# Three placements in a streaming mixer-and-experts kernel: where a register load stands, the order of a ring of buffers, and how far ahead splits run

## The chip, the cores and the metric

The kernel runs on one core of a Trainium2 chip. The metric is device microseconds (us) of one execution; the median of several runs is given. All times inside an execution come from one profiled execution and are counted from the start of its span.

## The reference, cut to what matters

One layer of a streaming encoder for 512 frames of 1024 features, in float32. Three mixers (differential attention, a gated delta rule, a diagonal state-space model) read one input projection; one output projection and a layer norm follow. Then a router picks, for each frame, one group of four experts and two experts in it, and the chosen experts of 16 gated MLPs are summed:

```python
def hier_moe(h, w_grp, b_grp, w_exp, b_exp, w1, w3, w2):
    ...
    for e in range(N_EXPERTS):
        hid = jax.nn.silu(hf @ w1[e]) * (hf @ w3[e])
        out = out + comb[:, e:e + 1] * (hid @ w2[e]).astype(jnp.float32)
```

`comb` is zero but for two experts of each frame, so an expert needs only the frames that chose it. A last layer norm ends the layer.

## The kernel before, in words

**Two halves.** The first half (to about 480 us) is the mixers, the output projection, the first layer norm (its result goes to two DRAM tensors, `hdr` and `yd`) and the routing. The routing ends in `place`, which writes tables of frame numbers and weights (`tab`), the numbers of the experts in the order in which they will run (`placed`, inside the tile `sb16`), and `cnti`, the largest number of frames that any expert has left over after its list. The second half runs the 16 experts, each on a list of at most 128 frames (large) or 64 (small). Expert 0, 1 and 2 are large; the 13 others follow as SSLSLSSLSLSLL, S for small and L for large, so nine are large and seven small.

**Weights.** An expert has 12 chunks of 128x1024 float32 (512 KB): eight "up" chunks, four "down" chunks. All 192 are loaded in order by SyncE (SP) into a ring of 32 places, `NRAW`. A place is a fixed stretch of SBUF that belonged to tiles of the first half; its first load must wait until the last user of those tiles has finished. Which place is used first, second, and so on is the tuple `RING`. SP issues in program order, so one load that waits holds back all loads behind it. A later load into a place waits for the chunk that was there 32 loads before. Load 29 is made to wait for the first two gathers (`FIRST = 28`).

**Splits.** A chunk of a large expert is split on the chip into a high part (`e_hi`, ScalarE) and a low part (`e_lo`, VectorE); three matmuls with the high and low parts of the frames (`xth`, `xtl`) stand for one float32 product. Split chunks lie in a ring of eight tiles, that is four chunks (`NHL = 8`). Chunks of small experts are used as they are loaded. `ahead(i, casts)` is called before step `i` (one chunk of PE work) and writes loads and splits into the program; how many steps a split may precede its use is `casts + AHEAD`, with `casts` 4 (2 in the last 12 steps), and no more than four splits are ever waiting. ScalarE and VectorE execute their instructions in program order, so where a split is written decides what waits behind it: `hid` (the activation of the previous expert) and `xth` and `xtl` (the next expert's frames) are on the same two engines.

**Frames.** POOL gathers the frames of an expert from `hdr` (`xg`), TensorE turns them, and adds the result to `yd` by an indirect DMA (`yd<-y,tab`). The last two experts are added on the chip, before the last layer norm.

**The register load.** Lines 1859 and 1860 load `cnti` into a register of every engine and branch, where an expert has frames left, into code that handles them. The load is written at the end of the program, outside the parts whose order is fixed by hand; the scheduler puts it, on each engine, by what it depends on. It depends on the write of `cnti` in line 289.

Of the kernel before, what the change touches and what calls it, by code (L numbers as in the profile page):

```python
# [16 lines left out]
ALU = mybir.AluOpType  # L17
AX = mybir.AxisListType
# [23 lines left out]
NQ4 = 4  # L42
RING = (2, 8, 15, 14, 21, 13, 12, 11, 9, 10, 5, 29, 7, 30, 18, 31, 16, 17, 19, 20, 6, 27, 28, 0, 1, 3, 4, 22, 23, 24, 25, 26)
OHT = 20
HT = 9
PRE = (4, 4, 9)
# [2 lines left out]
LAG = 2  # L49
CASTS = 4  # L50
CASTS2 = 2
AHEAD = 4
SW = 12
POOL = 4
NORM = 'vvvv'
# [4 lines left out]
NE = 16  # L60
# [21 lines left out]
def tile_layer(ctx: ExitStack, tc: tile.TileContext, a, out):  # L82
    nc = tc.nc

    def tt(o, x, y, op, e=nc.vector):
        return e.tensor_tensor(o, x, y, op=op)  # L86

    def ts(o, x, s1, op0, s2=None, op1=None, e=nc.vector):
        if op1 is None:
            return e.tensor_scalar(o, x, s1, None, op0=op0)  # L90
        return e.tensor_scalar(o, x, s1, s2, op0=op0, op1=op1)  # L91

    def stt(o, x, s, y, op0, op1):
        return nc.vector.scalar_tensor_tensor(o, x, s, y, op0=op0, op1=op1)  # L94
# [7 lines left out]
    def mm(o, l, r, start=True, stop=True):  # L102
        return nc.tensor.matmul(o, l, r, start=start, stop=stop)  # L103
# [34 lines left out]
    def ones_tile(shape, name, v=1.0):  # L138
        o = const.tile(shape, F32, name=name)
        nc.gpsimd.memset(o, v)  # L140
        return o
# [24 lines left out]
    sb16 = ones_tile([P, P], "sb16")  # L166
# [41 lines left out]
    cnti = const.tile([P, 1], I32, name="cnti")  # L208
# [24 lines left out]
        nc.vector.tensor_reduce(tab[1], p, axis=AX.X, op=ALU.add)  # L233


    more0, half2 = sb16[:, 0:NE], sb16[:, 32:33]
    placed = sb16.bitcast(I32)[:, 16:16 + ND]

    fold2 = stri
# [17 lines left out]
    def place(p, ct, pd, a, b):  # L257

        key, sl, red = a[:, 0:NE], a[:, 16:48].rearrange("p (x e) -> p x e", x=2), a[:, 64:64 + 2 * ND]
        rank, no = a[:, 96:96 + ND], a[:, 112:112 + NE]  # L260
        red = red.rearrange("p (x r) -> p x r", x=2)
        gt = a[:, 128:128 + ND * ND].rearrange("p (r e) -> p r e", e=ND)
        oh = a[:, 300:300 + ND * ND].rearrange("p (r e) -> p r e", e=ND)
        x = b[:, 0:2 * ND * ND].rearrange("p (x r e) -> p x r e", x=2, e=ND)
        sq, dyn = [P, ND, ND], slice(NS, NE)
        stt(key, ct, 16.0, i16, ALU.mult, ALU.subtract)
        tt(gt, key[:, None, dyn].to_broadcast(sq), key[:, dyn, None].to_broadcast(sq), ALU.is_gt)
        nc.vector.tensor_reduce(rank, gt, axis=AX.X, op=ALU.add)
        tt(oh, i16[:, 0:ND, None].to_broadcast(sq), rank[:, None, :].to_broadcast(sq), ALU.is_equal)
        tt(gt, oh, i16[:, None, dyn].to_broadcast(sq), ALU.mult)  # L270
        nc.vector.tensor_reduce(no[:, 0:ND], gt, axis=AX.X, op=ALU.add)
        nc.vector.tensor_copy(placed, no[:, 0:ND])
        ts(more0[:, dyn], rank, NL - 0.5, ALU.is_gt, float(SL - P), ALU.mult)
        for q, c in enumerate((slice(0, 2), slice(2, 5))):
            nc.vector.tensor_reduce(sl[:, q], p[:, :, c], axis=AX.X, op=ALU.add)
        mm(pd[:, 0:2 * NE], fold2, a[:, 16:48])
        ts(tab[0][:, 2:NS], sl[:, 0, 2:NS], 4096.0, ALU.add)
        nc.vector.tensor_copy(tab[1][:, 0:NS], sl[:, 1, 0:NS])
        pd = pd[:, 0:2 * NE].rearrange("p (x e) -> p x e", x=2)
        for r, y in ((slice(0, NL), sl), (slice(NL, ND), pd)):  # L280
            n = [P, 2, r.stop - r.start, ND]
            tt(x[:, :, r], y[:, :, None, dyn].to_broadcast(n), oh[:, None, r].to_broadcast(n), ALU.mult)
        nc.vector.tensor_reduce(red, x, axis=AX.X, op=ALU.add)
        ts(tab[0][:, NS:NS + NL], red[:, 0, 0:NL], 4096.0, ALU.add)
        ts(tab[0][:, NS + NL:], red[:, 0, NL:], 2.0, ALU.mult, half2, ALU.add)
        nc.vector.tensor_copy(tab[1][:, NS:], red[:, 1])
        tt(no, ct, more0, ALU.subtract)
        nc.vector.tensor_reduce(key[:, 0:1], no, axis=AX.X, op=ALU.max)
        nc.vector.tensor_copy(cnti, key[:, 0:1])


    def rsqrt(o, x, n, pool, eps, scale=1.0):
# [1170 lines left out]
    def halves(p):  # L1463
        return [p[:, 0:512], p[:, 512:D]]
# [3 lines left out]
    def traw(dt=F32):  # L1468
        nraw[0] += 1
        return rp[RING[(nraw[0] - 1) % NRAW]].tile([P, D], dt, name="e_raw", tag="raw")  # L1470

# [24 lines left out]
    def at(i, e):  # L1496
        return tab[i][:, column[e]:column[e] + 1]
# [20 lines left out]
    def turn_x(xg, e=0):  # L1518
        if small[e]:
            p = psT()  # L1520
            for j in range(4):
                nc.tensor.transpose(p[:, j * P:(j + 1) * P], xg[:, j * P:(j + 1) * P], ident)
            x = exs("xth", F32, 2)
            act(x, p, AF.Copy)
            return x
        return [turn(xg[:, i * 512:(i + 1) * 512], "xt", 2) for i in range(2)]
# [62 lines left out]
    def gather_for(e):  # L1589
        return gather(xgs[e % 2][:, 0:512] if small[e] else xgs[e % 2], at(0, e), 1 + small[e])  # L1590
# [24 lines left out]
    def ahead(i, casts):  # L1615
        while len(raws) < min(i + NRAW + 1, N):
            raws.append(traw())
            x = nc.sync.dma_start(raws[-1], weights(*steps[len(raws) - 1]))
            if len(raws) == FIRST + 1:

                for y in first:
                    tc.add_manual_dep(x.ins, y.ins.name, mybir.DependencyInfo(
                        mybir.DependencyClass.Sync, mybir.DependencyReason.DATA), reason="room")
        while len(ws) < min(i + casts + AHEAD, N):
            n = len(ws)
            if small[steps[n][0]]:
                ws.append(raws[n])
            elif n < i + casts or (nsplit[0] < nused[0] + casts and n < N - SW):
                ws.append(split(raws[n]))
                nsplit[0] += 1  # L1630
            else:
                break

    def step(i):
        e, c = steps[i]
        b = e % 2
        nused[0] += not small[e]
        if c < 8:
            if c == 0:
                pp[e] = psA(b)  # L1640
                if e + 2 < NE:
                    gather_for(e + 2)
            if small[e]:
                if c % 2:
                    up2(pp[e][0], xts[e], c // 2, ws[i - 1:i + 1])
            else:
                up(pp[e][c % 2], xts[e], c, ws[i])
                if c == 6:
                    hid[e] = hidden(pp[e])
            if c == 7:  # L1650
                if small[e]:
                    hid[e] = exs("hid", F32)
                    act(hid[e][0:SL], pp[e][0][0:SL], AF.Silu)
                    tt(hid[e][0:SL], pp[e][0][SL:P], hid[e][0:SL], ALU.mult)
                else:
                    tt(hid[e], pp[e][1], hid[e], ALU.mult)
                if e + 1 < NE:
                    xts[e + 1] = turn_x(xgs[(e + 1) % 2], e + 1)
                if e == 0:
                    turn_h(e)  # L1660
        else:
            if c == 8:
                pys[e] = psA(1 - b) if e == NE - 1 else psS()
            if small[e]:
                down2(pys[e][0], hts[e], c - 8, ws[i])
            else:
                down(pys[e], hts[e], c - 8, ws[i])
            if e == NE - 2 and c == HT:
                turn_h(e + 1)
            if c == 11:  # L1670
                if e + 1 < NE - 1:
                    turn_h(e + 1)
                if e < NE - 2:
                    (finish2 if small[e] else finish)(pys[e][0] if small[e] else pys[e], at(1, e), at(0, e))
                else:
                    y_parts(e)
# [17 lines left out]
    with tc.manual_schedule():  # L1694
        first.extend(gather_for(e) for e in range(2))
        ahead(0, CASTS)
        xts[0] = turn_x(xgs[0])
        for i in range(N - 4):
            ahead(i + 1, CASTS if i < N - SW else CASTS2)
            step(i)  # L1700
            if i == N - OHT:
                io = traw()[:, 0:S]
                gp.iota(io, pattern=[[1, S]], base=0, channel_multiplier=0, allow_small_or_imprecise_dtypes=True)
                oht.extend(halves(traw(F32R)))
                for j in range(2):
                    nc.vector.tensor_copy(li[j], at(0, NE - 2 + j))
                    ts(oht[j], io, li[j], ALU.is_equal)


    with tc.manual_schedule():  # L1710
# [265 lines left out]
```

## Time and profile before

| what | value |
|---|---|
| median of 3 runs | 814.47 us (812.86 to 816.69) |
| the profiled execution's own time | 810.5 us |
| its span, first to last instruction | 808.8 us |
| mean granted TensorE clock | 0.908 of full |
| TensorE matmuls busy | 695.3 us (86%) |
| VectorE (DVE) busy | 526.0 us (65%) |
| ScalarE (ACT) busy | 354.7 us (44%) |

The shares are means over two halves with different limits, so they say little by themselves. What limits a stretch has to be read from that stretch: which wait ends last there, and whether the DMA engines are full or empty.

### The profile page before, as it was taken

The numbers are of one execution on the slowest core, as the hardware profiler recorded it, in microseconds if no ns is written. First come the engines' busy times: TensorE is split into PE (matmuls) and PEld (weight loads), VectorE is DVE, ScalarE is ACT, GpSimd is POOL, SyncE is SP. The second block draws the span as 40 slices with busy tenths as digits, with TensorE's granted clock in tenths as the row PEclk, the third lists the DMA queues.
The fourth block names the chain that finished last, engine by engine and source line by source line (L and its number), as shares of the span: only waits on it lengthen the run. The fifth ranks groups of instructions, "written<-read, shape, count | busy, mean of one in ns | idle before, by whom it ended". The sixth has DMA issues, their size and how long they took to land. (4 is left out here: it accounts for less than half of the span.)

```text
span 808.8 us, 10863 instructions
## 1 busy us (share of the span) xinstructions
PE 695.3 (86%) x3568; PEld 504.5 (62%) x3568; DVE 526.0 (65%) x1405; ACT 354.7 (44%) x582; POOL 97.4 (12%) x140
## 2 busy tenths in 40 slices
PE   0999939997997999998999656899899859989793
PEld 0677827875885766676877555685556326736661
DVE  6999896678534455667568885792544233816866
ACT  2678625532115221545323205674544333726643
POOL 6010000000000011110000020012212102211022
PEclk9999969998979999596899756999999989999897
DMA  6133212121012575263000249999999999999822
GB/s 216 64 111 103 81 42 78 41 79 31 22 49 69 149 177 170 64 196 105 1 0 1 105 149 401 419 404 399 359 398 390 391 382 383 388 368 385 330 94 108
DMA packets 54272, 155.77 MB, mean 193 GB/s; under 512 B 13502, under 2 KB 13758, under 8 KB 54208
## 3 DMA queue, kind: packets, MB, share of 16 engines
q1 hardware_dynamic: 38960, 124.26, 39.8%
q0 software_dynamic: 8192, 18.86, 8.9%
q10 hardware_dynamic: 7056, 11.88, 4.8%
q8 instruction: 30, 0.49, 0.2%
q14 instruction: 34, 0.28, 0.1%
HBM read 139.98 MB, written 18.61 MB: 196 GB/s over the span
## 5 line engine op out<-in xcount | busy, mean ns | idle before, releaser
L86 DVE TENSOR_TENSOR e_lo<-e_raw,e_hi 128x1024 fp32r<-128x1024 f32 x108 | 131.4, 1239 | 93.6 <-ACT e_hi L97 91.3
L97 ACT ACTIVATE e_hi<-e_raw 128x1024 fp32r<-128x1024 f32 x108 | 112.6, 1060 | 89.3 <-DMA e_raw<-in_moe_w_dram 65.7
L103 PE MATMUL pA<-hTh,w_lo 128*128 128x512 f32 x184 | 76.3, 416 | 12.3 <-DVE w_lo L86 12.3
L103 PE MATMUL pA<-hTh,w_hi 128*128 128x512 f32 x184 | 77.5, 421 | 2.5 <-DVE cv L94 1.1
L103 PE MATMUL pA<-hTl,w_hi 128*128 128x512 f32 x184 | 74.6, 406 | 0.0
L103 PE MATMUL pA<-e_hi,xth 128*128 128x512 f32 x144 | 61.2, 425 | 6.2 <-ACT xth L97 6.2
L103 PE MATMUL pA<-e_hi,xtl 128*128 128x512 f32 x144 | 60.3, 419 | 0.6 <-DVE xtl L86 0.6
L103 PE MATMUL pA<-e_lo,xth 128*128 128x512 f32 x144 | 59.7, 415 | 0.6 <-DVE e_lo L86 0.6
L103 PE MATMUL pA<-e_raw,xth 128*64 128x512 f32 x224 | 53.9, 598 | 2.1 <-DMA e_raw<-in_moe_w_dram 2.1
L103 PEld LDWEIGHTS pA<-hTh,w_lo 128*128 128x128 f32 x184 | 36.1, 196 | 20.4 <-DVE w_lo L86 12.9
L1486 POOL DMA_INDIRECT yd__140<-y,tab x14 | 23.2, 1660 | 202.2 <-ACT y L97 202.2
L97 ACT ACTIVATE w_hi<-w_raw 128x1024 fp32r<-128x1024 f32 x29 | 30.6, 1055 | 33.8 <-PE pA L103 25.0
L103 PEld LDWEIGHTS pA<-hTh,w_hi 128*128 128x128 f32 x184 | 36.0, 196 | 12.5 <-issue 2.1
L103 PEld LDWEIGHTS pA<-hTl,w_hi 128*128 128x128 f32 x184 | 35.8, 195 | 7.6 <-issue 0.7
L103 PEld LDWEIGHTS pA<-e_raw,xth 128*64 128x64 f32 x224 | 16.8, 136 | 34.0 <-issue 23.1
L103 PEld LDWEIGHTS pA<-e_hi,xth 128*128 128x128 f32 x144 | 29.5, 205 | 13.3 <-ACT xth L97 6.6
L86 DVE TENSOR_TENSOR w_lo<-w_raw,w_hi 128x1024 fp32r<-128x1024 f32 x29 | 35.3, 1220 | 2.4 <-ACT w_hi L97 2.3
L103 PEld LDWEIGHTS pA<-e_lo,xth 128*128 128x128 f32 x144 | 29.4, 204 | 7.6 <-DVE e_lo L86 1.0
L103 PEld LDWEIGHTS pA<-e_hi,xtl 128*128 128x128 f32 x144 | 29.4, 204 | 7.2 <-DVE xtl L86 1.1
L1201 DVE TENSOR_REDUCE nm<-pA 128x1 f32<-128x128 f32 (+3 forms) x48 | 22.9, 484 | 13.8 <-PE pA L103 9.0
L97 ACT ACTIVATE pe<-pA,nm 128x128 f32<-128x128 f32 (+3 forms) x48 | 25.0, 527 | 11.9 <-DVE nm L1201 7.2
L97 ACT ACT_TABLE_LOAD x21 | 26.9, 1283 | 6.7 <-DVE cv L94 6.4
(525 smaller groups left out, 1475.1 us busy)
## 6 DMA issues: line engine op xcount, KB each, us to landing
e_raw<-in_moe_w_dram SPq DMA_DIRECT2D x192, 512.0 KB, 11.5
w_raw<-in_w_cm_dram SPq DMA_DIRECT2D x12, 512.0 KB, 3.4
w_raw<-in_w_cm_dram ACTq DMA_DIRECT2D x11, 512.0 KB, 3.5
qks<-qkd POOLq DMA_DIRECT2D x18, 256.0 KB, 4.0
qkd<-qk SPq DMA_DIRECT2D x6, 512.0 KB, 2.8
h0d<-x SPq DMA_DIRECT2D x4, 512.0 KB, 3.4
w_raw<-in_w_out_dram SPq DMA_DIRECT2D x4, 512.0 KB, 3.6
w_raw<-in_w_out_dram ACTq DMA_DIRECT2D x4, 512.0 KB, 5.9
```

Source lines behind the costliest of these rows:

```text
L86: return e.tensor_tensor(o, x, y, op=op)
L97: return nc.scalar.activation(o, x, f, **kw)
L103: return nc.tensor.matmul(o, l, r, start=start, stop=stop)
L1201: nc.vector.tensor_reduce(nm[:, c:c + 1], pc[c][:, 0:nk], axis=AX.X, op=ALU.max, negate=True)
L1486: nc.gpsimd.indirect_dma_start(out=rows_of(yd, n), out_offset=bass.IndirectOffsetOnAxis(ap=idx, axis=0), in_=y, in_offset=None, bounds_che ...
```

## The change

Three edits. The largest leftover count is kept as a float (`most`) where it is worked out, and the cast into `cnti` is written in the expert loop, 20 steps before its end. `RING` is put in another order: places 5, 3 and 6 go back, 3 and 6 to the end. `AHEAD` goes from 4 to 0, so a split may precede its use by `casts` steps, four in most of the loop.

```diff
-RING = (2, 8, 15, 14, 21, 13, 12, 11, 9, 10, 5, 29, 7, 30, 18, 31, 16, 17, 19, 20, 6, 27, 28, 0, 1, 3, 4, 22, 23, 24, 25, 26)
+RING = (2, 8, 15, 14, 21, 13, 12, 11, 9, 10, 29, 7, 30, 18, 31, 16, 17, 19, 20, 27, 28, 0, 1, 4, 5, 22, 23, 24, 25, 26, 3, 6)
...
-AHEAD = 4
+AHEAD = 0
...
-    more0, half2 = sb16[:, 0:NE], sb16[:, 32:33]
+    more0, half2, most = sb16[:, 0:NE], sb16[:, 32:33], sb16[:, 33:34]
...
-        nc.vector.tensor_reduce(key[:, 0:1], no, axis=AX.X, op=ALU.max)
-        nc.vector.tensor_copy(cnti, key[:, 0:1])
+        nc.vector.tensor_reduce(most, no, axis=AX.X, op=ALU.max)
...
                     ts(oht[j], io, li[j], ALU.is_equal)
+                nc.vector.tensor_copy(cnti, most)
```

**On SP**, around the first expert loads, the program before has the rows below. `e_raw` is a chunk of expert weights, `g` the first layer norm's factors, `sb` the tile with the experts' order.

```order
L1250 DMA w_raw<-in_w_out_dram 128x1024 x2
L1291 DMA g_3759<-in_ln_g_dram 128x1024
L1859 TENSOR_LOAD cnti
L1859 ISA x2
L1618 DMA e_raw<-in_moe_w_dram 128x1024 x32
L1611 TENSOR_LOAD sb_91
```

The same place in the changed program (its line numbers are one lower up to the loop's end):

```order
L1249 DMA w_raw<-in_w_out_dram 128x1024 x2
L1290 DMA g_3759<-in_ln_g_dram 128x1024
L1617 DMA e_raw<-in_moe_w_dram 128x1024 x32
L1610 TENSOR_LOAD sb_91
L1617 ISA
```

The load of `cnti` no longer stands ahead of the chunk loads. It is found again at SP's end, behind the last loads (`yd` read back, the last layer norm's factors) and ahead of the stores of the output:

```order
L1714 DMA e_raw<-yd__140 128x1024 x4
L1717 DMA e_raw<-in_ln_g_dram 128x1024
L1717 DMA e_raw<-in_ln_b_dram 128x1024
L1859 TENSOR_LOAD cnti
L1859 ISA x2
L1813 DMA out_dram<-e_raw 128x512 x2
```

**On ScalarE**, where the sixth expert, a large one, follows two small ones, the program before has these rows; `e_hi` is a split, `xth` the next expert's frames, `hhh` the turned activation, `y` the scaled result.

```order
L97 ACTIVATE hid<-pA 64x512
L97 ACTIVATE xth<-pT 128x512
L97 ACTIVATE hhh<-pT 128x256
L97 ACTIVATE y<-pS,tab_136 128x512 x2
L97 ACTIVATE e_hi<-e_raw 128x1024 x4
L97 ACTIVATE hid<-pA 64x512
L97 ACTIVATE xth<-pT 128x512 x2
L97 ACTIVATE hhh<-pT 128x256
```

And the changed program:

```order
L97 ACTIVATE hid<-pA 64x512
L97 ACTIVATE xth<-pT 128x512
L97 ACTIVATE hhh<-pT 128x256
L97 ACTIVATE y<-pS,tab_136 128x512 x2
L97 ACTIVATE hid<-pA 64x512
L97 ACTIVATE xth<-pT 128x512 x2
L97 ACTIVATE e_hi<-e_raw 128x1024 x4
L97 ACTIVATE hhh<-pT 128x256
```

Four splits go behind `hid` and `xth`. The same move is made at one more place, the large expert after the next two small ones in a row; and at the last expert, which is large and follows a large one, three splits go behind `xth`. On VectorE the `e_lo` of these splits go behind `hid` and `xtl` in the same way. At the other large experts the splits stood behind `hid` and `xth` already. TensorE's and POOL's order does not change.

## Rows read from the trace of the kernel before

**Rows 1.** Waits of SP's queue: engine, line, releaser, us in total, times, longest.

```profile
SPq L1859 <- DVE cnti L289: 103.7, 1, 103.7
```

**Rows 2.** Timeline of SP: start us, us, engine, line, operation, count.

```profile
481.97 37.79 SPq L1618 DMA_DIRECT2D e_raw<-in_moe_w_dram  x33
...
499.94 29.72 SPq L1618 DMA_DIRECT2D e_raw<-in_moe_w_dram  x24
```

**Rows 3.** Window: us, busy PE, PEld, DVE, ACT, POOL, granted clock, DMA share, GB/s.

```profile
408.00:451.00 43.00, 40.01 (x227) 32.22 (x226) 31.85 (x94) 15.19 (x44) 1.08 (x2) 1.00 0.06 25
```

**Rows 4.** Timeline: last uses of tiles that lay in the ring's places.

```profile
410.10 0.39 PE L103 MATMUL pA<-w_lo,yTb 128*128 128x512 f32 x1
...
454.01 1.05 PE L103 MATMUL pA<-w_hl,yTt 128*128 128x512 f32 x2
...
469.65 1.28 DVE L94 SCALAR_TENSOR_TENSOR xo<-xo,ln_r,g 128x1024 f32<-128x1024 f32 x1
```

**Rows 5.** POOL's DMAs, 380 to 560 us (median us to landing), and the first gather.

```profile
hdr<-xo POOLq DMA_DIRECT2D x4, 512.0 KB, 3.0
...
xg<-hdr,tab POOLq DMA_INDIRECT x6, 7.2
...
471.23 0.53 POOL L1344 DMA_DIRECT2D hdr<-xo  x1 [5.18 <-DVE lg L94]
...
478.96 1.10 POOL L1481 DMA_INDIRECT xg<-hdr,tab  x1 [4.83 <-DVE cb L86]
...
480.37 1.02 POOL L1481 DMA_INDIRECT xg<-hdr,tab  x1 [0.30 <-issue]
```

**Rows 6.** Groups by line: the same VectorE operation in the second and the first half.

```profile
L86 DVE TENSOR_TENSOR e_lo<-e_raw,e_hi 128x1024 fp32r<-128x1024 f32 x108 | 131.4, 1239 | 93.6 <-ACT e_hi L97 91.3
...
L86 DVE TENSOR_TENSOR w_lo<-w_raw,w_hi 128x1024 fp32r<-128x1024 f32 x29 | 35.3, 1220 | 2.4 <-ACT w_hi L97 2.3
```

**Rows 7.** Timeline around the first expert's first matmuls, with idle time before each.

```profile
486.10 0.17 DVE L286 COPY tab<-pla 128x13 f32<-128x13 f32 x1
...
487.24 1.06 ACT L97 ACTIVATE e_hi<-e_raw 128x1024 fp32r<-128x1024 f32 x1 [12.06 <-DMA e_raw<-in_moe_w_dram]
...
489.92 3.72 DVE L86 TENSOR_TENSOR e_lo<-e_raw,e_hi 128x1024 fp32r<-128x1024 f32 x3 [0.36 <-ACT e_hi L97]
...
493.56 1.28 DVE L86 TENSOR_TENSOR xtl<-pT,xth 128x512 fp32r<-128x512 f32 x2
...
494.29 0.80 PE L103 MATMUL pA<-e_hi,xtl 128*128 128x512 f32 x1 [0.58 <-DVE xtl L86]
```

**Rows 8.** Waits of TensorE, 486 to 790 us: releaser, us in total, times, longest.

```profile
PE pT L1572 <- DVE xtl L86: 10.0, 2, 7.7
PE pT L1515 <- DVE xtl L86: 7.5, 2, 4.1
...
PE pA L103 <- DMA e_raw<-in_moe_w_dram: 2.1, 4, 1.1
PE pS L103 <- ACT e_hi L97: 1.9, 2, 1.2
PE pS L103 <- DMA e_raw<-in_moe_w_dram: 1.7, 2, 1.1
```

**Rows 9.** Group by line: down matmuls of large experts, idle before them at the end.

```profile
L103 PE MATMUL pS<-e_lo,hhh 128*128 128x512 f32 x64 | 25.4, 398 | 1.4 <-DVE e_lo L86 1.4
```

**Rows 10.** Timeline of ScalarE and TensorE at the longest of these waits.

```profile
658.14 1.06 ACT L97 ACTIVATE e_hi<-e_raw 128x1024 fp32r<-128x1024 f32 x1 [13.38 <-DMA e_raw<-in_moe_w_dram]
...
665.60 0.69 PE L1572 MATMUL pT<-ident,hid 64*128 64x64 f32 x4 [7.66 <-DVE xtl L86]
```

**Rows 11.** Windows at half clock after three of the waits; columns as in rows 3.

```profile
577.80:581.20 3.40, 3.40 (x10) 2.63 (x9) 1.23 (x1) 1.31 (x2) 2.56 (x2) 0.50 0.98 377
...
659.70:670.00 10.30, 4.40 (x13) 3.51 (x14) 6.47 (x8) 6.33 (x9) 2.07 (x2) 0.50 1.02 407
...
751.90:758.70 6.80, 5.78 (x16) 4.72 (x17) 5.61 (x10) 2.66 (x4) 1.77 (x1) 0.50 1.02 414
```

## The prediction, on record before the changed kernel ran

> **What bounds the kernel now.** I read the waits of SP's queue first, because SP issues all loads of expert weights. One wait stands out: SP's load of `cnti` waits 103.7 us for VectorE [rows 1]. All expert loads stand behind it in SP's program, and the timeline of SP shows the result: the first is issued at 481.97 us, and from then on SP issues one as fast as the DMA engines take it, 24 in 29.72 us, 1.238 us each [rows 2]. So while SP waits, the DMA engines are nearly empty: from 408 to 451 us their share is 0.06 [rows 3].
>
> Next come the waits in the second half. TensorE stands still for ScalarE and VectorE, and ScalarE's own wait behind that is for a chunk: at 658.14 us a split has waited 13.38 us for its DMA, and TensorE starts again only at 665.60 us, after 7.66 us, when `xtl`, which stands behind the splits, is done [rows 10]. So the second half is held by the stream of loads in some places and by TensorE's own work in the others. Removing the first can bring no more than TensorE's idle time there and what follows from it.
>
> **The register load.** It leaves the place ahead of the chunk loads. Where does the stall go? Each load then waits for its place to be left by the first half. I took from the program's semaphore counts which instruction each of the first 28 loads waits for, and from the trace when that ends. The first may go earlier than all others; loads 2 to 9 wait for matmuls of the output projection, the last of which ends at 410.10 + 0.39 = 410.5 us; loads up to 26 for later ones, up to 454.01 + 1.05 = 455.1 us; load 28 for the first layer norm's last operation, 469.65 + 1.28 = 470.9 us [rows 4]. At 1.238 us each, 28 loads take 34.7 us, and the window from 408 to 451 us alone has 43 us with empty engines [rows 3]. So all 28 lie in SBUF by about 474 us. Load 29 waits for the first two gathers: the second is issued at 480.37 us and gathers land 7.2 us after issue [rows 5], so at 487.6 us. Before, 28 loads after 481.97 us ended at 481.97 + 34.7 = 516.7 us. **The stream gets 516.7 - 487.6 = 29.1 us ahead.** That is not yet the gain, only its upper bound as far as loads go.
>
> On SP the load of `cnti` now precedes the stores of the output, and its cast sits on VectorE 20 steps earlier than the end; it waits for nothing by then and lies under the last expert's matmuls. I count both as nothing. If that cover were gone, it would be one load, 481.97 less the end of the wait, about 1 us.
>
> **The start of the experts.** Now the first four splits wait for the DMA; ScalarE has been idle for 12.06 us before the first [rows 7], so with the chunks there all four `e_hi` fit into idle time. VectorE is next: its `e_lo` stand behind the last routing operation, which ends at 486.10 + 0.17 = 486.27 us. Four `e_lo` at 3.72 / 3 = 1.24 us and one `xtl` at 1.28 / 2 = 0.64 us end at 491.9 us; before, the matmul that needs this `xtl` began at 494.29 us [rows 7]. **Gain 2.4 us**, and not the 5 that the DMA's lateness suggests: VectorE is late next.
>
> **The waits inside.** TensorE's waits between 486 and 790 us that go back to a late chunk are 10.0 us in front of small turns, 2.1 and 1.7 us for chunks used unsplit, 1.9 us for `e_hi` [rows 8], 1.4 us for `e_lo` [rows 9], and the longer of the two waits in front of large turns, 4.1 us; the other one, 7.5 - 4.1 = 3.4 us [rows 8], comes in the first experts, where the chunks were there in time, and I leave it. **Sum 21.2 us.**
>
> **The clock.** After three of these waits the granted clock is 0.50, that is 1.2 instead of 2.4 GHz, and TensorE is busy 3.40, 4.40 and 5.78 us in those windows [rows 11]. What is done in them takes twice as long, so half of 13.6 us comes back if the waits are gone: **6.8 us**. The bounds are 0, if other short waits keep the clock low, and 6.8; I take all of it, as no wait over 1.2 us would be left near these places.
>
> **The splits.** `AHEAD` 0 moves splits at three places, where the three longest waits stand (4.1 us, and the two that make up the 10.0 us): ScalarE no longer blocks `xth` with a split that waits for a chunk. With chunks early this blocking is gone anyway, so I count no second gain. It has a price: the first `e_hi` and `e_lo` of the next large expert now come after `xtl`. If TensorE had to wait for both in full, that is 1.06 + 1.24 = 2.3 us at each of three places, 6.9 us [rows 7]; if the previous expert's down matmuls cover them, nothing. I take a third, **2.4 us lost**, since those matmuls take longer than one split.
>
> **The ring's order.** Places 3 and 6 hold the routing's scratch tables, whose last reader ends at 486.27 us [rows 7]. In the old order they come 26th and 21st, so load 21 and the seven early ones behind it would wait with SP until then: 8 x 1.238 = 9.9 us of the lead would be missing. In the new order they come last, behind load 28. This is no gain beside the one above but a part of the 29.1 us.
>
> **Contention.** The loads now run beside the first half's last work. VectorE's same operation takes 1239 ns beside full DMA engines and 1220 ns in the first half [rows 6]: 1.6% of the 31.85 us that VectorE is busy from 408 to 451 us [rows 3] is 0.5 us, the upper end; the lower is nothing. I take nothing. A DMA beside a DMA is another matter. POOL's writes of `hdr` land 3.0 us after issue; the last is issued at 471.23 us and the first gather, which reads `hdr`, at 478.96 us, when VectorE has its list ready [rows 5]. So 7.7 - 3.0 = 4.7 us are spare, and only load 28, 1.24 us, meets this write.
> The Trainium skill speaks against the change here: its page "DMA: Bandwidth & Descriptors", section "Issuing engines are not separate DMA queues", says that DMAs of all issuing engines run on the same 16 engines and interleave. By that rule a write of `hdr` beside a load would land later, and with two loads beside each of the four writes the routing could start to wait; by the row, even a doubled landing time of the last write, 6.0 us, stays within 7.7 us. The sum would be the same by both.
>
> **The sum.** 2.4 + 21.2 + 6.8 - 2.4 = **28.0 us**. That is under the 29.1 us by which the stream gets ahead, so TensorE is the bound and the stream just keeps up. From the profiled execution's 810.5 us this leaves 782.5 us. The median of the runs shown is 4 us above the profiled execution, so I predict 814.47 - 28.0 = **786.5 us** as a median.
>
> **Rivals.**
> - *The ring fills and the stream bounds again.* 28 of 32 places are full when the first three experts start. Their chunks need at least VectorE's 1.24 us of split and other work beside, so the stream, at 1.238 us, may run into full places and lose its lead. For it: gain and lead lie 1 us apart. Against it: the loads already share the engines with scatters and gathers, which slows them more than TensorE's pace does. Were a third of the lead lost, the gain is 29.1 x 2/3 = 19.4 us: **795 us**.
> - *The waits go, the clock stays.* Other short waits hold the clock down, and the last wait of 4.1 us remains, as the one of 3.4 us does: 28.0 - 6.8 - 4.1 = 17.1 us, **797 us**.
> - *The change does not do what it says.* One of the first loads waits for a place that is freed only with the routing, and all behind it wait too: **814 us**. Against it speak the times in [rows 4], if the semaphore counts are read rightly.
> - *Slower: the splits come too late.* With four chunks instead of eight, TensorE would wait at each of the six large experts among the last 13 for the four splits that used to be ready, 1.06 + 4 x 1.24 = 6.0 us [rows 7], 36 us in all. Against the gain without the split term, 30.4 us, that is a loss of 5.6 us: **820 us**. It decides from 30.4 / 6 = 5.1 us of wait at each. Against it: at most four split chunks fit in their ring in both kernels, and the order changes at three places only.
> - *Better.* The 3.4 us go too, and the lead grows because the gathers land sooner without loads beside them: 34 us, **780 us**.
>
> **Numbers.** Forecast 0.60 (by itself 782 to 792), ring 0.13, clock 0.13, better 0.07, no effect 0.04, slower 0.03. The range from 779 to 799 us takes in the ring and the clock case and most of the better one, and leaves out the last two and the edges. A measurement of this kernel can tell about 0.5%, 4 us, from no change: faster 0.93, within 0.04, slower 0.03.
>
> **What would show it.** The ninth expert load is issued near 411 us and not near 490; the DMA share from 408 to 451 us rises from 0.06 to above 0.6; SP's longest wait is for a place and not for `cnti`. TensorE's 7.66 us wait is gone, and the two others with it; the windows after them have clock 1.00. The second matmul of the first expert starts near 492 us. The tail from the last expert's down matmuls on is as long as before. I am wrong if ScalarE still waits for chunks after 600 us (then the stream bounds), if TensorE waits for `e_lo` at the large experts (then the splits do), or if the span up to the first expert grows (then it is contention).

## The result

The changed kernel takes 784.66 us, the median of 4 runs (781.14 to 787.67), beside 815.49 us for the kernel before on the same chip: a ratio of 0.9625, 95% interval 0.9571 to 0.9678. The forecast was 786.5 us. The profiled execution took 786.6 us, its span 784.7. Some executions of these kernels take a per cent or more longer at a lower granted clock; the ratios leave them out, the medians in the table below do not, and the profiles of two kernels there ("ring of 28" and "`xtl` first") are of such executions.

The medians differ by 30.8 us and the two profiled spans by 24.1. The first half holds the same work in both, yet in this profile it ends 2.9 us later than in that of before. So the two traces are compared from one instruction on that both have, the last routing matmul. Timeline of TensorE before, and below it after: start, duration, operation, idle time before it and what ended it.

```profile
484.29 0.63 PE L103 MATMUL pG<-pla,stri 128*128 128x32 f32 x2 [0.40 <-DVE pla L275]
...
492.92 0.80 PE L103 MATMUL pA<-e_hi,xth 128*128 128x512 f32 x1 [6.24 <-ACT xth L97]
```

```profile
487.17 0.64 PE L103 MATMUL pG<-pla,stri 128*128 128x32 f32 x2 [0.40 <-DVE pla L275]
...
489.40 0.79 PE L103 MATMUL pA<-e_hi,xth 128*128 128x512 f32 x1
494.33 0.80 PE L103 MATMUL pA<-e_hi,xtl 128*128 128x512 f32 x1 [4.14 <-DVE xtl L86]
```

From that matmul to the end of the span it was 808.8 - 484.29 = 324.5 us and is 784.7 - 487.17 = 297.5 us: **27.0 us less**. I call this the expert time, and use it for all runs below; a second profile of the changed kernel gives 297.6 us.

**Where the loads went.** SP's waits after (the wait for `cnti`, [rows 1], is not among them), and then how many expert loads SP had issued by 490, 515 and 660 us (the number behind the first "x" of a line), after and below it before.

```profile
SPq L1617 <- DMA e_raw<-in_moe_w_dram: 111.4, 118, 3.1
...
SPq L1617 <- PE pA L103: 51.8, 24, 19.6
SPq L1617 <- DVE e_lo L86: 36.9, 35, 4.9
```

```profile
L1617 SPq DMA_DIRECT2D e_raw<-in_moe_w_dram x32: 327/380/1068, 391.1 to 489.6; - x32
...
L1617 SPq DMA_DIRECT2D e_raw<-in_moe_w_dram x44: 327/338/1068, 391.1 to 510.3; - x44
...
L1617 SPq DMA_DIRECT2D e_raw<-in_moe_w_dram x138: 327/333/1068, 391.1 to 659.6; - x138
```

```profile
L1618 SPq DMA_DIRECT2D e_raw<-in_moe_w_dram x10: 328/504/1090, 482.0 to 488.7; - x10
...
L1618 SPq DMA_DIRECT2D e_raw<-in_moe_w_dram x29: 327/328/1090, 482.0 to 513.7; - x29
...
L1618 SPq DMA_DIRECT2D e_raw<-in_moe_w_dram x126: 327/333/1090, 482.0 to 659.4; - x126
```

The changed kernel is ahead by 22 loads at 490 us, by 15 at 515, and by 12 at 660: a lead that is won in the first half and partly lost again, most of it by 515 us. The windows show why (columns as in rows 3).

```profile
408.00:451.00 43.00, 41.80 (x233) 33.62 (x231) 31.38 (x82) 15.01 (x41) 1.08 (x2) 1.00 0.63 231
451.00:490.00 39.00, 22.75 (x162) 19.75 (x161) 34.42 (x188) 10.44 (x32) 7.29 (x11) 0.59 0.63 237
490.00:540.00 50.00, 42.52 (x182) 34.70 (x182) 38.90 (x39) 33.31 (x39) 6.81 (x4) 0.88 0.89 315
540.00:600.00 60.00, 60.00 (x289) 34.66 (x288) 30.37 (x31) 30.40 (x41) 14.04 (x8) 1.00 1.00 374
600.00:735.00 135.00, 129.10 (x586) 77.62 (x585) 69.29 (x72) 69.48 (x91) 26.06 (x16) 1.00 1.01 382
...
516.00:775.00 259.00, 247.50 (x1119) 156.87 (x1117) 152.55 (x171) 144.20 (x193) 57.71 (x35) 1.00 0.92 341
```

From 408 to 451 us the DMA share is 0.63 instead of 0.06 [rows 3]. From 490 to 540 it is 0.89: the ring is full and SP waits for places. From 540 us on it is 1.00: from here the stream goes as fast as the DMA engines can, and TensorE catches up with it. The granted clock is 1.00 from 516 to 775 us.

**Where TensorE and ScalarE wait now.** TensorE's waits from 486 to 780 us; below, ScalarE's for chunks after 600 us.

```profile
PE pA L103 <- DVE xtl L86: 4.1, 1, 4.1
PE pT L1514 <- DVE xtl L86: 3.3, 1, 3.3
PE pA L103 <- DVE e_lo L86: 3.2, 5, 1.2
PE pA L103 <- DMA e_raw<-in_moe_w_dram: 1.7, 2, 1.6
PE pS L103 <- DVE e_lo L86: 1.6, 3, 0.5
PE pS L103 <- ACT e_hi L97: 1.0, 2, 0.7
```

```profile
ACT e_hi L97 <- DMA e_raw<-in_moe_w_dram: 23.0, 14, 10.4
```

The waits in front of small turns (10.0 us) and the large one of 4.1 us [rows 8] are gone; the 4.1 us that stand here are the start. But ScalarE still waits 14 times for a chunk, 23.0 us in all after 600 us (44.9 before). The prediction named this as a sign that it is wrong. So the time came near the forecast, and a reason behind it needs testing.

### The profile page after: what moved, and what is told of

The parts are those of the page before. It is cut to its first block, busy times and chain, and to the rows that moved or that the text cites. A ratio compares the mean times of both kernels' runs of the same rounds, so it can differ in the third digit from the quotient of the medians.

```text
span 784.7 us, 10853 instructions
## 1 busy us (share of the span) xinstructions
PE 689.7 (88%) x3565; PEld 502.2 (64%) x3568; DVE 523.9 (67%) x1405; ACT 352.6 (45%) x582; POOL 102.8 (13%) x140
## 5 line engine op out<-in xcount | busy, mean ns | idle before, releaser
L86 DVE TENSOR_TENSOR e_lo<-e_raw,e_hi 128x1024 fp32r<-128x1024 f32 x108 | 129.2, 1237 | 39.0 <-ACT e_hi L97 36.6
L97 ACT ACTIVATE e_hi<-e_raw 128x1024 fp32r<-128x1024 f32 x108 | 110.5, 1059 | 45.0 <-DMA e_raw<-in_moe_w_dram 23.0
L103 PE MATMUL pA<-e_hi,xtl 128*128 128x512 f32 x144 | 57.8, 401 | 4.1 <-DVE xtl L86 4.1
L103 PE MATMUL pA<-e_lo,xth 128*128 128x512 f32 x144 | 58.0, 403 | 1.5 <-DVE e_lo L86 1.5
L103 PE MATMUL pA<-e_hi,xth 128*128 128x512 f32 x144 | 58.7, 408 | 0.0
L103 PE MATMUL pA<-e_raw,xth 128*64 128x512 f32 x224 | 52.9, 598 | 1.9 <-DMA e_raw<-in_moe_w_dram 1.7
L1485 POOL DMA_INDIRECT yd__140<-y,tab x14 | 25.8, 1841 | 177.6 <-ACT y L97 177.6
L86 DVE TENSOR_TENSOR hid<-pA,hid 128x512 f32<-128x512 f32 (+1 forms) x16 | 11.0, 690 | 43.8 <-ACT hid L97 27.6
L103 PEld LDWEIGHTS pA<-e_hi,xtl 128*128 128x128 f32 x144 | 28.0, 194 | 10.4 <-DVE xtl L86 4.6
```

The costliest lines, as they stand in the source:

```text
L97: return nc.scalar.activation(o, x, f, **kw)
L1485: nc.gpsimd.indirect_dma_start(out=rows_of(yd, n), out_offset=bass.IndirectOffsetOnAxis(ap=idx, axis=0), in_=y, in_offset=None, bounds_che ...
```

## The experiments

All times are medians of six executions (four in the first row of the changed kernel, twelve for "load in front again" and "ring of 28, places moved"); each ratio is to the kernel before on the same chip.

| kernel | us | ratio, 95% interval | expert time |
|---|---|---|---|
| before | 812 to 816 | 1 | 324.5 |
| changed | 784.66 | 0.9625 (0.9571 to 0.9678) | 297.5 |
| changed, again | 787.93 | 0.9665 (0.9610 to 0.9719) | 297.6 |
| load in front again | 809.16 | 0.9952 (0.9916 to 0.9988) | 318.6 |
| load at the end alone | 794.16 | 0.9740 (0.9680 to 0.9800) | 304.0 |
| changed, `AHEAD` 4 | 796.23 | 0.9742 (0.9668 to 0.9815) | 302.2 |
| changed, old ring order | 791.59 | 0.9669 (0.9590 to 0.9749) | 297.3 |
| changed, half of the loads | 776.57 | 0.9534 (0.9478 to 0.9591) | 285.8 |
| half of the loads, `AHEAD` 4 | 778.47 | 0.9532 (0.9486 to 0.9578) | 286.2 |
| ring of 28, places moved | 809.09 | 0.9920 (0.9884 to 0.9955) | 319.0 |
| ring of 28 | 797.50 | 0.9750 (0.9698 to 0.9802) | 303.0 |
| `xtl` first | 785.13 | 0.9615 (0.9558 to 0.9671) | 294.5 |
| `xtl` first, turn late | 786.89 | 0.9671 (0.9622 to 0.9721) | 294.9 |
| `xtl` first, ring of 34 | 781.42 | 0.9607 (0.9557 to 0.9656) | 292.3 |

The expert time is the span of the profiled execution less the start of the last routing matmul, one profile each. "Changed, again" came as expected (782 to 790 us).

**The register load in front again.** Ring order and `AHEAD` 0 stay.

```diff
-        nc.vector.tensor_reduce(most, no, axis=AX.X, op=ALU.max)
+        nc.vector.tensor_reduce(key[:, 0:1], no, axis=AX.X, op=ALU.max)
+        nc.vector.tensor_copy(cnti, key[:, 0:1])
...
-                nc.vector.tensor_copy(cnti, most)
```

Expected: 

> The changed kernel with the register load back in front of all expert loads; the new ring order and AHEAD 0 stay. Theory (the place of the load carries the gain): SP waits some 104 us for VectorE again, the first expert load is issued near 482 us, the window from 408 to 451 us has a DMA share near 0.06, and the time is that of before within 4 us, 811 to 817 us. Rival (the later splits carry a part, since ScalarE no longer stands in front of a late chunk with the next transpose behind it): most of the 10.0 us of waits in front of small turns and their half clock come back without any early load, so 800 to 806 us.

Most of the gain is gone: 809.16 us, between the two ranges expected, and an expert time of 318.6 us, between 297.5 (changed) and 324.5 (before). So the load's place is worth 318.6 - 297.5 = 21.1 us. The 5.9 us that are left come from `AHEAD` 0 (or the ring's order) with all chunks late. Waits of SP, and of TensorE from 486 to 780 us:

```profile
SPq L1859 <- DVE cnti L289: 101.0, 1, 101.0
```

```profile
PE pA L103 <- ACT xth L97: 7.0, 1, 7.0
PE pA L103 <- DMA e_raw<-in_moe_w_dram: 4.6, 8, 1.6
PE pA L103 <- DVE e_lo L86: 4.4, 7, 1.2
PE pT L1515 <- DVE xtl L86: 3.3, 1, 3.3
```

No long wait in front of a turn stands here, although SP waits for `cnti` as before: these waits, 10.0 and 4.1 us in [rows 8], go away with `AHEAD` 0 alone. The lateness turns into many shorter waits for chunks instead. The rival's mechanism is there, at about half of the size that it was given. That the 5.9 us are the splits' and not the ring order's is argued from these waits, not tested by a run of its own.

**The load at the end alone, and each of the other two edits undone.** Three kernels: old ring order with `AHEAD` 4; the changed kernel with `AHEAD` 4; the changed kernel with the old ring order.

```diff
-RING = (2, 8, 15, 14, 21, 13, 12, 11, 9, 10, 29, 7, 30, 18, 31, 16, 17, 19, 20, 27, 28, 0, 1, 4, 5, 22, 23, 24, 25, 26, 3, 6)
+RING = (2, 8, 15, 14, 21, 13, 12, 11, 9, 10, 5, 29, 7, 30, 18, 31, 16, 17, 19, 20, 6, 27, 28, 0, 1, 3, 4, 22, 23, 24, 25, 26)
...
-AHEAD = 0
+AHEAD = 4
```

Expected of both together (the load alone): 

> Only the register load moves; old ring order and AHEAD 4. The 21st expert load has to wait for the routing (486 us), so 20 loads lie in SBUF early and eight are missing, about 10 us of the lead; loads from the 29th on land near 501 us, between the 491 of the changed kernel and the 524 of the kernel before. Theory (the lead is cut anyway once the ring of 32 places is full, to 16 to 18 us by the 128th load): the 10 us matter little, 785 to 790 us. Rival (the lead is carried to the end, as in the prediction's step on the ring's order): 10 us of it missing give 793 to 798 us.

Expected of `AHEAD` 4: 

> The changed kernel with AHEAD 4 again. By the prediction's term for the splits (AHEAD 0 costs 2.4 us) this is 2 us faster than the changed kernel, 781 to 784 us. Theory after the trace (the splits' order is worth nothing while chunks are early, and the stream is late by some us only between 670 and 735 us): the same within 3 us, 783 to 788 us. Rival (ScalarE blocked by a split that waits for its chunk, in front of a transpose, where its longest wait for a chunk is now 10.4 us): 4 us or more slower than the changed kernel, 789 us or above.

Expected of the old ring order: 

> The changed kernel with the old ring order; the load sits at the end and AHEAD is 0. The 21st expert load waits until about 486 us. Theory (the full ring cuts the lead anyway): 785 to 789 us, within 0.5% of the changed kernel. Rival (the 9.9 us of lead that the ring's order is worth by the prediction come back one for one): 793 to 797 us.

With `AHEAD` 0 the old ring order costs nothing that can be seen: an expert time of 297.3 us beside 297.5, and a ratio inside the interval of the changed kernel (its median, 791.59 us, lies between the two ranges expected). With `AHEAD` 4 it is 304.0 beside 302.2 us, with equal ratios. The windows and the loads issued by 490 and 515 us, with the old order and `AHEAD` 0:

```profile
408.00:451.00 43.00, 41.80 (x234) 33.67 (x233) 31.33 (x82) 15.15 (x41) 1.08 (x2) 1.00 0.35 135
...
490.00:540.00 50.00, 42.53 (x183) 34.67 (x183) 39.12 (x39) 33.52 (x39) 6.83 (x4) 0.88 1.02 404
```

```profile
L1617 SPq DMA_DIRECT2D e_raw<-in_moe_w_dram x23: 327/458/1487, 394.0 to 489.7; - x23
...
L1617 SPq DMA_DIRECT2D e_raw<-in_moe_w_dram x44: 327/372/1487, 394.0 to 512.7; - x44
```

At 490 us nine loads are missing, where eight (9.9 us) were worked out. By 515 us they are made up: 44 in both, since the new order's ring is full and has to wait, while with the old order the DMA engines go on at 1.02. A lead beyond what the ring holds is not kept.

`AHEAD` 4 costs 302.2 - 297.5 = 4.7 us of expert time with the new ring order, and 304.0 - 297.3 = 6.7 us with the old one. The times (0.9742 beside 0.9625 and 0.9665) point the same way, with intervals that overlap. The trace says where. ScalarE and TensorE with `AHEAD` 4:

```profile
731.25 1.06 ACT L97 ACTIVATE e_hi<-e_raw 128x1024 fp32r<-128x1024 f32 x1 [6.68 <-DMA e_raw<-in_moe_w_dram]
732.50 1.06 ACT L97 ACTIVATE e_hi<-e_raw 128x1024 fp32r<-128x1024 f32 x1 [0.19 <-DMA e_raw<-in_moe_w_dram]
733.73 1.06 ACT L97 ACTIVATE e_hi<-e_raw 128x1024 fp32r<-128x1024 f32 x1 [0.17 <-DMA e_raw<-in_moe_w_dram]
734.70 1.06 ACT L97 ACTIVATE xth<-pT 128x512 fp32r<-128x512 f32 x2
...
737.30 1.12 PE L1514 MATMUL pT<-ident,hid 128*128 128x128 f32 x4 [4.18 <-DVE xtl L86]
```

The same place with `AHEAD` 0:

```profile
726.91 1.08 ACT L97 ACTIVATE xth<-pT 128x512 fp32r<-128x512 f32 x2 [4.57 <-PE pT L1514]
728.92 1.06 ACT L97 ACTIVATE e_hi<-e_raw 128x1024 fp32r<-128x1024 f32 x1 [0.93 <-DMA e_raw<-in_moe_w_dram]
...
730.83 0.66 PE L1514 MATMUL pT<-ident,hid 128*128 128x128 f32 x4
```

With `AHEAD` 4 `xth` stands behind three splits whose chunks land late, and TensorE waits 4.18 us for the `xtl` made from it. With `AHEAD` 0 `xth` goes when its transposes are done, and the wait for the chunks lies under TensorE's work. So the rival that was named for `AHEAD` 4 holds (796.23 us, 789 or above expected), and neither the prediction's term nor my first reading of the trace does. The load alone took 794.16 us, outside of the 785 to 790 us that I expected and inside its rival's range. But the rival's reason, that the lead missing with the old order is carried to the end, is not what the traces show: the load alone is 304.0 - 297.5 = 6.5 us behind the changed kernel, and with the old order `AHEAD` 0 alone gives 6.7 us.

**Half of the loads.** Is TensorE or the stream the bound in the changed kernel? After the 32nd load every second one is left out, and the chunk before it is used twice (so half of the later weights are left out; the other engines have the same work).

```diff
+            if len(raws) >= NRAW and len(raws) % 2:
+                raws.append(raws[-1])
+                continue
             raws.append(traw())
```

Expected: 

> The changed kernel, with every second load after the first 32 left out: the chunk before it is used twice (so half of the experts' weights are wrong, and the work of all other engines is the same). Theory (from 540 us on the DMA engines are full, and the waits of TensorE between 671 and 735 us come from late chunks): these waits, 5.3 us in all, are gone with the splits' waits for a DMA, and the time falls by 4 to 7 us, to 778 to 782 us. Rival (TensorE and the splits of the large experts bound there, whatever the loads do): within 1.5 us of the changed kernel.

The expert time falls to 285.8 us, 11.7 less, about twice what was expected. The waits of TensorE that the view names for late chunks and late splits explain half. Over the same matmuls, from the first with `xtl` to the last expert's end, the window of this kernel is

```profile
496.00:745.60 249.60, 244.52 (x1136) 161.12 (x1136) 154.87 (x153) 147.57 (x183) 52.54 (x30) 0.99 0.65 213
```

where the changed kernel has 261.40 us with 250.39 busy (the line stands in the next section): 5.9 us less idle time and 5.9 us less busy time. The granted clock is 1.00 in both from 22 us into these windows on, and before that they are alike. What shortens the busy time shows in who waited for a load in the changed kernel: TensorE's weight loads (PEld) do too.

```profile
who waited for it (us, times):
  ACT e_hi L97: 23.0, 14
  PEld pA L103: 7.9, 14
  PEld pS L103: 2.5, 9
  PE pA L103: 1.7, 2
```

With half of the loads nobody waits for one, and the 224 matmuls of unsplit chunks (`pA<-e_raw,xth`), which overlap one another, take 49.6 us as a group instead of 52.9 in these windows. The 10.4 us of the weight loads cannot simply be added to the idle time, since weight loads overlap matmuls too. So in the changed kernel the stream, not TensorE, bounds the experts for these 12 us.

**Half of the loads with `AHEAD` 4**, to see whether the splits' order costs anything when no chunk is late.

```diff
-AHEAD = 0
+AHEAD = 4
```

Expected: 

> Half of the loads after the 32nd left out as before (the chunk ahead used twice), and AHEAD 4. With the full loads AHEAD 4 left two waits of TensorE in front of large turns, 1.9 and 4.2 us. Theory (a split that waits for its chunk stands in front of the transposed x on ScalarE): without late chunks these two waits are gone too, and the time is that of the half loads with AHEAD 0 within 2 us, 774 to 779 us. Rival (the splits in front of the turn take ScalarE's and VectorE's time by themselves): the two waits stay, and it is 4 to 8 us slower than that, 781 to 785 us.

The expert time is 286.2 us beside 285.8, the median 778.47 us as expected, and no wait in front of a turn is left but the one in the first experts:

```profile
PE pT L1514 <- DVE xtl L86: 3.3, 1, 3.3
```

So the order of the splits matters here only where a chunk is late: the rival falls, and the condition in the prediction ("with chunks early this blocking is gone anyway") is right. What was wrong is that the chunks are early.

**A ring of 28 places.** The first try set `NRAW` to 28 and used the first 28 entries of the order.

```diff
-NRAW = 32
+NRAW = 28
...
-    rp = [t2.enter_context(tc.tile_pool(name="rp%d" % i, bufs=1, reuse_waits="tile")) for i in range(NRAW)]
+    rp = [t2.enter_context(tc.tile_pool(name="rp%d" % i, bufs=1, reuse_waits="tile")) for i in range(32)]
```

Expected: 

> The changed kernel with a ring of 28 places instead of 32; the first 28 loads are the same. Theory (the lead is what the full ring allows, and the DMA engines can't win it back later): four places less are 4 x 1.24 = 5 us less lead, chunks land about 5 us later from the 56th load on, and the time grows by 3 to 7 us, to 788 to 792 us. Rival (the DMA engines' rate alone sets the end, and the ring is large enough): less than 2 us slower.

It took 809.09 us, outside of both expectations, for a reason of its own. SP's waits:

```profile
SPq L1617 <- DVE pla L283: 97.2, 1, 97.2
```

The second load waited 97.2 us for the routing's `pla`, and all loads behind it waited with it. I take it that the four pools that were never used took no room, so that the others moved onto other scratch; the wait is measured, this reason is inferred. That is the prediction's third rival ("does not do what it says"), by accident: an early register load is worth nothing if one early place is freed late. An expert time of 319.0 us, beside 318.6 with the load in front, shows the same loss.

The second try leaves the first 32 loads as they are and uses 28 places from the 33rd on.

```diff
-        return rp[RING[(nraw[0] - 1) % NRAW]].tile([P, D], dt, name="e_raw", tag="raw")
+        return rp[RING[nraw[0] - 1 if nraw[0] <= NRAW else (nraw[0] - NRAW - 1) % 28]].tile([P, D], dt, name="e_raw", tag="raw")
...
-        while len(raws) < min(i + NRAW + 1, N):
+        while len(raws) < min(i + (29 if i else NRAW + 1), N):
```

Expected: 

> The ring of 28 places once more, now with all places where they were: the first 32 loads as in the changed kernel, from the 33rd on only 28 of the places are used in turn. (In the first try the four unused places were not set up at all, so all others lay elsewhere, and the second load waited 97 us for the routing.) Theory (what is left of the lead is what the ring holds, and the full DMA engines can't win it back): chunks land some 5 us later from the 64th load on, and the time grows by 3 to 7 us, to 788 to 795 us. Rival (the ring is large enough): within 2 us of the changed kernel.

797.50 us, a ratio of 0.9750, 0.9 to 1.3% above the changed kernel's two ratios; the expert time is 5.5 us longer. The median is above the expected range (788 to 795 us), and the expert time is longer by the middle of the 3 to 7 us expected. So the sign is shown, and the size is not settled within a few us. A smaller ring leaves less of the lead.

**`xtl` first, and the turn late.** The wait of 4.14 us at the start is VectorE's: `xtl` stands behind four `e_lo`.

```diff
-        tt(lo, raw, f32(hi), ALU.subtract, e=e)
+        if late is None:
+            tt(lo, raw, f32(hi), ALU.subtract, e=e)
+        else:
+            late.append((lo, raw, hi))
...
-        ahead(0, CASTS)
+        late = []
+        ahead(0, CASTS, late)
         xts[0] = turn_x(xgs[0])
+        for lo, raw, hi in late:
+            tt(lo, raw, f32(hi), ALU.subtract)
```

Expected: 

> The changed kernel with VectorE's four first e_lo written behind the first expert's xtl instead of in front of it. Now xtl waits 5 us for them, and TensorE stands still from 490.2 to 494.3 us. Theory (the wait is VectorE's order, and the places that come free earlier let the stream follow): the wait falls from 4.1 to below 1.5 us, and the time by 2 to 4 us, to 781 to 783 us. Rival (the DMA engines bound from 540 us on, so what is won at the start is waited for later): the wait at the start goes, the waits between 671 and 735 us grow by as much, and the time is the same within 1 us.

The expert time is 294.5 us, 3.0 less. The first `e_lo` matmul comes 5.5 us behind the last routing matmul instead of 7.8, here and in the kernel with the turn late, which has the same start. The median, 785.13 us, misses the expected 781 to 783 us and is not to be told from the changed kernel's. The late turn writes the first expert's `turn_h` behind the second expert's first chunk:

```diff
+TURN0 = 0
...
+            if e == 1 and c == TURN0:
+                turn_h(0)
...
-                if e == 0:
-                    turn_h(e)
```

Expected: 

> The first expert's xtl in front of its e_lo, as in the run with xtl first, and the turn of its hidden layer written behind the first chunk of the second expert, so that TensorE has matmuls while ScalarE and VectorE finish the hidden layer (now 3.3 us of wait). Theory (both waits are order alone, and places that come free earlier let the loads follow): 5 to 6 us less than the changed kernel, 779 to 783 us. Rival (the DMA engines, full from 540 us on, take it back): the two waits go, those between 671 and 735 us grow, and the time is within 2 us of the changed kernel.

An expert time of 294.9 us: nothing beyond `xtl` first, and the median, 786.89 us, is that of the changed kernel. The 3.3 us of wait turn into two others, of 0.83 and 2.05 us, for the second expert's `xth` and `xtl`, which now stand in the way. TensorE's waits between 660 and 740 us stay as they were, 6.0 us beside 5.8. So it is the order, and not the DMA engines, that takes this back; the expected 5 to 6 us fell short.

**A ring of 34 places**, with `xtl` first. SBUF has room for two more.

```diff
-NRAW = 32
+NRAW = 34
...
-        ... 25, 26, 3, 6)
+        ... 25, 26, 32, 33, 3, 6)
```

Expected: 

> The changed kernel with the first expert's xtl in front of its four e_lo, as before, and with two places more in the ring, 34 (the 29th to 34th loads take the places 25, 26, 32, 33, 3 and 6). Theory (chunks are late after 600 us because the ring fills, and four places less cost 5.5 us of the time from the last routing matmul on): two places more give back 2 to 3 us of it; with xtl first, which was worth 3.0 us there, that time falls from 297.5 us to 291 to 293 us, and the whole to 779 to 783 us. Rival (the DMA engines' rate, full from 540 us on, holds the end, and what the ring takes up earlier is not to be had): the time from the last routing matmul on stays at 294 to 295 us, as with xtl first alone.

781.42 us, ratio 0.9607, the lowest of all kernels that compute everything; an expert time of 292.3 us, 2.2 less than with `xtl` first alone and 5.2 less than the changed kernel. Its interval overlaps the changed kernel's, so the gain stands on one trace of each kernel, where it has the expected size.

## Why the prediction came out right

**The sum came close: 28.0 us forecast, 27.0 us of expert time.** In part that is luck, as its steps show:

- *The signs named.* The DMA share, the clock, the small turns and SP's longest wait among the chunk loads, which is for a place (19.6 us), came as forecast, and so did the lead: counted from the last routing matmul, the 29th load is issued 28.6 us earlier (513.7 us before, 488.0 after; 29.1 forecast). The tail too: from the last matmul of the last expert that waits for an `e_lo` it is 29.1 us to the end before (808.8 - 779.7) and 29.0 after (784.7 - 755.7).
- *The start*, 2.4 us. From the last routing matmul to the first matmul with `xtl` it was 494.29 - 484.29 = 10.0 us and is 494.33 - 487.17 = 7.2: 2.8 us. Right, VectorE's `e_lo` being late next as worked out.
- *The waits inside*, 21.2 us. Windows over the same matmuls, up to the last expert's end:

```profile
494.30:779.70 285.40, 258.37 (x1135) 166.87 (x1135) 155.50 (x152) 148.72 (x183) 46.62 (x30) 0.95 0.98 377
```

```profile
494.30:755.70 261.40, 250.39 (x1136) 161.94 (x1136) 153.88 (x153) 146.82 (x183) 51.64 (x30) 0.98 0.98 364
```

 TensorE's idle time falls from 27.0 to 11.0 us: **16.0 us, not 21.2**. Waits for chunks (1.7 us), for `e_hi` (1.0) and for `e_lo` (4.8, where the kernel before had 3.8) are left, since the stream is late again after 600 us. These 16.0 us hold what the splits' order did, too: the sum set 21.2 - 2.4 = 18.8 us against them.
- *The clock*, 6.8 us. The busy time falls by 258.37 - 250.39 = 8.0 us, with a granted clock of 1.00 behind 516 us. Right, the upper bound. The 1.2 us beyond it need not be the clock: with half of the loads the busy time fell at equal clock, too.
- *The splits*, 2.4 us lost (a third of 6.9 is 2.3). **Wrong in sign.** `AHEAD` 0 gains 4.7 us beside `AHEAD` 4, up to 6.7 with the old ring. The step that failed is "with chunks early this blocking is gone anyway, so I count no second gain": the chunks are not early at two of the three places, where waits of 1.9 and 4.2 us stand with `AHEAD` 4. The price, a wait for the first `e_lo` behind `xtl`, shows up at none of the three places at more than 0.6 us.
- *The ring's order*, 9.9 us of the lead. With the old order nine loads are missing at 490 us and made up by 515; in expert time the order is worth nothing with `AHEAD` 0 (0.2 us the other way) and 1.8 us with `AHEAD` 4. A lead of loads was right, a part of the gain it was not.
- *Contention*, nothing. From SP's load of `g` to the last routing matmul it is 107.3 us before and 107.4 after (SP, before and after):

```profile
377.01 0.33 SPq L1291 DMA_DIRECT2D g<-in_ln_g_dram  x1
```

```profile
379.82 0.33 SPq L1290 DMA_DIRECT2D g<-in_ln_g_dram  x1
```

 The writes of `hdr` do land later, 6.2 us instead of 3.0 [rows 5]. The trace agrees with the rule of the Trainium skill that DMAs of all issuing engines run on the same 16 engines and interleave (page "DMA: Bandwidth & Descriptors", section "Issuing engines are not separate DMA queues"). The last write is issued at 474.10 us and the gather at 481.84, the same 7.7 us apart: the spare time covered it.

```profile
hdr<-xo POOLq DMA_DIRECT2D x4, 512.0 KB, 6.2
...
474.10 0.53 POOL L1343 DMA_DIRECT2D hdr<-xo  x1 [5.18 <-DVE lg L94]
...
481.84 1.10 POOL L1480 DMA_INDIRECT xg<-hdr,tab  x1 [4.83 <-DVE cb L86]
```

- *"TensorE is the bound and the stream just keeps up."* **Wrong.** This is the first rival's mechanism: the ring fills, the lead falls from 22 loads to 12, and 11.7 us are left that half of the loads sets free. The rival took 28.0 - 19.4 = 8.6 us off the gain for it. With `AHEAD` 4 the load and the ring's order bring 324.5 - 302.2 = 22.3 us, a loss of that size, and `AHEAD` 0 moves the late chunks out of the way of the turns.

So two errors met: the load and the ring's order bring 22.3 us, not the 30.4 of the sum without its split term, and the splits add 4.7 instead of taking 2.4. Asked for the change without `AHEAD` 0, the same sum would have missed by 8 us.

## What to carry to other kernels

In this kernel a prefetch that starts earlier was worth what its buffers hold, not how much earlier it starts. Elsewhere, count the places, see when they are all full, and ask whether the DMA engines have idle time after that. If they are full from there on, the consumers can catch up, and a chunk is late again before the end, as here. Then it matters what stands behind a wait for it in an engine's program: work with a late input belongs behind work whose input is there.

## What was not expected of the hardware

Behind the point where the lead is used up, waits for a chunk show on TensorE's weight loads (10.4 us) more than on its matmuls (1.7 us); the busy share of PE hides about half of what the stream costs (5.9 of the 11.7 us that half of the loads set free). And the first half, with the same work in all kernels, is not equally long: the last routing matmul starts between 482.0 and 501.9 us, and the granted clocks differ. From 200 to 300 us the clock is 0.94 in the profile of the changed kernel and 0.91 with `AHEAD` 4, where that matmul starts 2.4 us later. Changes of 1% in the second half are told from one another by a time that begins there.
